# Gate scatter of a product-key expert layer: one-hots for two tokens side by side in place of four

## The chip, the cores and the metric

The kernel runs on one core of one Trainium2 chip. Its time is the device time of one execution, in microseconds (us); several executions are timed and their median is given. TensorE multiplies matrices, VectorE, ScalarE and GpSimd work element by element, and the SyncE queue issues most of the DMAs. The engines run side by side and wait for one another by semaphores. Each engine works its instructions off in the order in which they stand in its own queue. TensorE first loads a matmul's stationary operand (its weights) and then streams the columns of the moving operand past it; the profile lists the loads apart, as PEld.

## The reference

One residual decoder layer on 256 tokens of 1024 features, in float32: a token-mixing part (two causal attention branches), and a part that retrieves experts by product keys, then a norm. The change concerns the second. Each token has 8 heads; each head scores two sets of 128 sub-keys, and its 16 best pairs of sub-keys name 16 of 128 x 128 experts, with softmax gates. An expert is one neuron:

```
u = expert_u[ic]
hval = jnp.einsum('cd,chkd->chk', xc, u)
a = gc * jax.nn.gelu(hval, approximate=False)
out = jnp.einsum('chk,chkd->cd', a, expert_v[ic])
```

## The kernel before, in words

The kernel gathers no experts. It computes all 16384 neurons for all tokens, and multiplies each by the sum of the gates that its token gave to it, zero for most. The experts lie in 128 blocks of 128, block i holding those whose first sub-key is i. `up(i)` (L446) computes one block for all 256 tokens: a load of 512 KB from `u_t`, a split of these weights into two parts of a rounded four-byte type (`hi` on ScalarE, L83, and `lo` on VectorE, L84), and 24 matmuls of 128 x 128 weights with 256 columns (three products for each of eight slices of the features, L93, L96, L97). The last stage, `v_step`, multiplies the gated neurons with `v_e`, 128 blocks of 12 matmuls with 512 columns each.

The gates come from `route` (L456), which picks the experts on VectorE while the query projections and the first 42 blocks of `up` (`N_PRE`) run on TensorE. It leaves for each token its 128 slots (8 heads of 16) across the partitions: `slot_e` holds the two sub-key numbers of a slot, `slot_g` its gate as the sum of two fp16 numbers, a high and a low part.

`scatter(t4, done)` (L595) turns the slots of four tokens into a matrix of gates, 128 second sub-keys by 128 first ones for each token. On VectorE it compares `iota`, the numbers 0 to 127, with the slots of the four tokens at once; that gives both one-hots in `oh` (L602), and `gi` (L603) is the first one-hot times the two parts of the gate. Both tiles are [128, 2, 128, 4] in fp16: the four tokens lie innermost, next to each other, so the 128 columns of one token lie four elements, 8 bytes, apart. On TensorE each token takes two matmuls (L606), with `oh[:, 1, :, q]` as weights and `gi[:, part, :, q]` as the moving operand: 128 x 128 by 128 columns, eight for a scatter, into one PSUM bank. The bank is then multiplied into the neurons that are already there (L608, L611 on VectorE), or copied for those that come later (L613 on ScalarE), which `up_post` (L617) multiplies by the neuron afterwards (L624, L625).

There are 64 scatters (256 tokens in fours). They are called between the blocks 42 to 127 of `up`, about three for every four blocks, and those are the stretch from 388 to 697 us of the profile. Pools of two buffers each hold `oh`, `gi` and the PSUM banks; weights have three. The order within each engine's queue is laid down when the kernel is built, by the framework's scheduler from a modelled timeline, so a scatter's eight matmuls need not stand together in TensorE's queue.

Of the kernel before, what the change touches and what calls it, by code (L numbers as in the profile page):

```python
# [11 lines left out]
F16 = mybir.dt.float16  # L12
# [3 lines left out]
ALU = mybir.AluOpType  # L16
AX = mybir.AxisListType

P = 128
# [10 lines left out]
NK = 128  # L30
# [11 lines left out]
C_ID, C_IOTA, C_POS, C_KEEP = np.cumsum([0, P, P, NCAND]).tolist()  # L42
# [9 lines left out]
def body(ctx, tc, x, g_mix, w_fb, w_va, w_qk, w_gate, w_f, b_f, w_br, w_out, g_ffn, w_pq,  # L52
         keys_t, u_t, v_e, g_fin, c_keep, c_mix, c_rot, c_sel, out, dbg=None):
    nc = tc.nc
# [8 lines left out]
    def bank(tag):  # L63
        return psum.tile([P, 512], F32, name=tag)
# [34 lines left out]
    cst = cpool.tile([P, C_KEEP], F32, name="cst")  # L99
# [67 lines left out]
    def proj_t(src, xt, behind=None, tag="mm", late=False):  # L167
        w = split(src, behind)
        ps = bank(tag)[:, :S]
        if not late:  # L170
            for k in range(KD):
                mm3(ps, wk(w, k), [v[:, k] for v in xt], k == 0, k == KD - 1)
        else:

            for k in range(KD):
                for v in xt:
                    nc.tensor.matmul(ps, lhsT=wk(w, k)[0], rhs=v[:, k], start=k == 0 and v is xt[0], stop=False)  # L177
            for k in range(KD):
                nc.tensor.matmul(ps, lhsT=wk(w, k)[1], rhs=xt[0][:, k], start=False, stop=k == KD - 1)
        return ps  # L180


    with ExitStack() as fr:
# [5 lines left out]
        for t in range(NT):  # L189
            for n in range(2):  # L190
                sl = slice(n * 512, (n + 1) * 512)
# [23 lines left out]
        ps = bank("tp")[:HEADS, :S]  # L215
# [17 lines left out]
        for o in (0, 32, 64):  # L233
            part = ck[o:o + HEADS, P:]
# [149 lines left out]
        for j2 in range(KD // 2):  # L384
# [3 lines left out]
            for jj in range(2):  # L388
                j = 2 * j2 + jj
                pp = []  # L390
                for w, yt, tag in ((wb, ys[0], "mm"), (wa, ys[1], "py")):
                    ps = bank(tag)[:, :S]
# [40 lines left out]
    tk = ctx.enter_context(tc.tile_pool(name="tk", bufs=1))  # L433

    slot_e = tk.tile([P, 2, S], F16, name="slot_e")
    slot_g = tk.tile([P, 2, S], F16, name="slot_g")
    iota = tk.tile([P, NK, 4], F16, name="iota")
    nc.vector.tensor_copy(out=iota, in_=cst[:, C_IOTA:C_IOTA + P].unsqueeze(2).to_broadcast([P, NK, 4]))
    ew = ctx.enter_context(tc.tile_pool(name="ew", bufs=2))
    pre = ctx.enter_context(tc.tile_pool(name="pre", bufs=1))  # L440
    act = [pre.tile([P, N_PRE, S], F32, name="act0")]
# [109 lines left out]
    with ExitStack() as fr:  # L551
# [21 lines left out]
        for m in range(2 * PH):  # L573
            first = m < FIRST
            ps = proj_t(w_pq[m], xt2, (None if m == 0 else normed[0], normed[1]) if first else (qhs[m - FIRST], None), late=first)
# [19 lines left out]
    def scatter(t4, done):  # L595

        ps = bank("tp")
        sl = slice(t4 * 4, t4 * 4 + 4)
        wide = [P, 2, NK, 4]
        oh = ew.tile(wide, F16, name="oh")  # L600
        gi = ew.tile(wide, F16, name="gi")
        nc.vector.tensor_tensor(out=oh, in0=iota.unsqueeze(1).to_broadcast(wide), in1=slot_e[:, :, sl].unsqueeze(2).to_broadcast(wide), op=ALU.is_equal)  # L602
        nc.vector.tensor_tensor(out=gi, in0=oh[:, 0].unsqueeze(1).to_broadcast(wide), in1=slot_g[:, :, sl].unsqueeze(2).to_broadcast(wide), op=ALU.mult)  # L603
        for q in range(4):
            for part in range(2):
                nc.tensor.matmul(ps[:, q * NK:(q + 1) * NK], lhsT=oh[:, 1, :, q], rhs=gi[:, part, :, q], start=part == 0, stop=part == 1)  # L606
        pv = ps.rearrange("p (q i) -> p i q", i=NK)
        nc.vector.scalar_tensor_tensor(out=act[0][:, :, sl], in0=pv[:, :N_PRE], scalar=1.0 / G_SCALE, in1=act[0][:, :, sl], op0=ALU.mult, op1=ALU.mult)  # L608
        d = done - N_PRE
        if d > 0:  # L610
            nc.vector.scalar_tensor_tensor(out=act[1][:, :d, sl], in0=pv[:, N_PRE:done], scalar=1.0 / G_SCALE, in1=act[1][:, :d, sl], op0=ALU.mult, op1=ALU.mult)  # L611
        if done < NK:
            nc.scalar.mul(out=act[1][:, d:, sl], in_=pv[:, done:], mul=1.0 / G_SCALE)  # L613
# [15 lines left out]
    t4 = 0  # L629
    for i in range(N_PRE, NK):  # L630
        upto = -(-(i - N_PRE + 1) * n4 // (NK - N_PRE))
        while t4 < upto:
            scatter(t4, i)
            t4 += 1
        up_post(i, 4 * t4)
# [63 lines left out]
    for n, lo in enumerate((0, 256, 512, 768)):  # L699
        sl = slice(lo, lo + 256)  # L700
# [85 lines left out]
```

## Time and profile before

| | |
|---|---|
| time, median of 3 runs | 1054.86 us (1054.21 to 1056.71) |
| profiled execution | 1059.37 us, its span 1057.6 us |
| TensorE matmuls | busy 1040.5 us (98%), 7076 instructions |
| VectorE | busy 740.6 us (70%), 1479 instructions |
| ScalarE | busy 546.1 us (52%), 983 instructions |
| HBM | 167 GB/s over the span |

The span reaches from the first instruction to the last. Busy times are shares of it; matmuls overlap in their pipeline, so the length of one is more than the time from its start to the start of the next. "Idle before" is the time in which an engine stood still ahead of the instructions of a row, with what it waited for behind the arrow.

### The profile page before, as it was taken

How to read it: one execution, taken by the hardware profiler on the slowest of the kernel's cores; microseconds unless marked ns; L12 is line 12 of the kernel's file. 1: busy time of each engine (PE TensorE's matmuls, PEld its weight loads, DVE VectorE, ACT ScalarE, POOL GpSimd, SP SyncE). 2: the span in 40 equal slices, each digit the busy share in tenths (PEclk: the TensorE clock that was granted, in tenths of full speed). 3: DMA queues.
4: the chain of work that ended last, by engine and by line, in shares of the span. 5: the costliest groups of instructions: out<-in, count | busy, mean ns of one | idle time of the engine just before them, and what ended most of it. 6: DMA issues, size and time to landing. Idle time of an engine off the chain costs nothing.

```text
span 1057.6 us, 18493 instructions
## 1 busy us (share of the span) xinstructions
PE 1040.5 (98%) x7076; PEld 953.7 (90%) x7076; DVE 740.6 (70%) x1479; ACT 546.1 (52%) x983; POOL 6.9 (1%) x12
## 2 busy tenths in 40 slices
PE   7999999989999999999999999999999999999997
PEld 5888999989999999999999999998888888888886
DVE  4566546679999986677777788866566656656665
ACT  5555566454554544444444444455555555555554
POOL 1000000000000000000000000000000000000001
PEclk8999999999999999999999999999999999999999
DMA  6544435544566564545455444556666666666663
GB/s 206 172 139 118 123 120 175 186 169 151 167 190 189 177 186 150 158 142 155 146 151 149 146 152 142 157 163 197 189 193 198 192 190 195 196 190 193 198 193 126
DMA packets 49959, 177.84 MB, mean 168 GB/s; under 512 B 5752, under 2 KB 6648, under 8 KB 49744
## 3 DMA queue, kind: packets, MB, share of 16 engines
q1 hardware_dynamic: 49104, 175.62, 54.9%
q8 instruction: 55, 0.90, 0.4%
q10 hardware_dynamic: 432, 0.66, 0.2%
q0 software_dynamic: 336, 0.40, 0.2%
q14 instruction: 32, 0.26, 0.1%
HBM read 175.60 MB, written 1.05 MB: 167 GB/s over the span
## 4 chain that ended last, share of the span: by engine, by line
PE 95%; DVE 3%; DMA 1%; ACT 0%; issue 0%; SPq 0%; ACTq 0%
PE mm L93 16%; PE mm L96 15%; PE mm L97 15%; PE py L93 6%; PE py L97 6%; PE py L96 6%; PE tp L606 6%; PE sp L93 6%; PE sp L97 6%; PE sp L96 6%; PE sp L312 1%; PE mm L177 1%; DVE lo L84 1%; DMA cst<-in_c_keep_dram 1%; PE sp L580 1%; PE tp L327 1%
## 5 line engine op out<-in xcount | busy, mean ns | idle before, releaser
L84 DVE TENSOR_TENSOR lo<-raw,hi 128x1024 fp32r<-128x1024 f32 x328 | 400.2, 1221 | 145.7 <-ACT hi L83 143.8
L83 ACT CAST hi<-raw 128x1024 fp32r<-128x1024 f32 x328 | 344.8, 1053 | 256.2 <-PE mm L96 142.0
L93 PE MATMUL mm<-xt2h,hi 128*128 128x256 f32 x1128 | 325.8, 289 | 0.8 <-ACT act L588 0.8
L97 PE MATMUL mm<-xt2h,lo 128*128 128x256 f32 x1128 | 317.5, 281 | 0.5 <-DVE lo L84 0.5
L96 PE MATMUL mm<-xt2l,hi 128*128 128x256 f32 x1128 | 317.2, 281 | 0.0
L93 PEld LDWEIGHTS mm<-xt2h,hi 128*128 128x128 f32 x1128 | 214.3, 190 | 1.6 <-ACT act L588 1.0
L97 PEld LDWEIGHTS mm<-xt2h,lo 128*128 128x128 f32 x1128 | 212.7, 189 | 0.9 <-DVE lo L84 0.9
L96 PEld LDWEIGHTS mm<-xt2l,hi 128*128 128x128 f32 x1128 | 213.6, 189 | 0.0
L643 ACT CAST ah<-act 128x256 fp32r<-128x256 f32 x128 | 52.0, 407 | 95.2 <-PE sp L96 95.1
L644 DVE TENSOR_TENSOR al<-act,ah 128x256 fp32r<-128x256 f32 x128 | 54.3, 425 | 60.0 <-PE sp L97 59.1
L96 PE MATMUL py<-lo,ah 128*128 128x512 f32 x256 | 79.9, 390 | 0.0
L93 PE MATMUL py<-hi,ah 128*128 128x512 f32 x256 | 79.7, 390 | 0.0
L97 PE MATMUL py<-hi,al 128*128 128x512 f32 x256 | 79.6, 389 | 0.0
L96 PE MATMUL sp<-lo,ah 128*128 128x512 f32 x254 | 79.0, 389 | 0.0
L93 PE MATMUL sp<-hi,ah 128*128 128x512 f32 x254 | 78.9, 389 | 0.0
L97 PE MATMUL sp<-hi,al 128*128 128x512 f32 x254 | 78.7, 389 | 0.0
L606 PE MATMUL tp<-gi,oh 128*128 128x128 f16 x512 | 74.8, 296 | 0.0
L613 ACT ACTIVATE act<-tp 128x344 f32<-128x344 f32 (+31 forms) x64 | 20.3, 318 | 86.6 <-DVE act L611 80.8
L608 DVE SCALAR_TENSOR_TENSOR act<-tp,act 128x168 f32<-128x168 f32 x64 | 21.2, 332 | 56.1 <-PE tp L606 56.1
L93 PE MATMUL mm<-xt1h,hi 128*128 128x256 f32 x208 | 60.4, 290 | 0.0
L97 PE MATMUL mm<-xt1h,lo 128*128 128x256 f32 x208 | 59.5, 286 | 0.0
L96 PE MATMUL mm<-xt1l,hi 128*128 128x256 f32 x208 | 59.3, 285 | 0.0
(259 smaller groups left out, 1408.0 us busy)
## 6 DMA issues: line engine op xcount, KB each, us to landing
raw<-in_u_t_dram SPq DMA_DIRECT2D x128, 512.0 KB, 3.5
raw<-in_v_e_dram SPq DMA_DIRECT2D x128, 512.0 KB, 3.5
raw<-in_w_gate_dram SPq DMA_DIRECT2D x16, 512.0 KB, 3.6
raw<-in_w_pq_dram SPq DMA_DIRECT2D x16, 512.0 KB, 3.7
raw<-in_w_fb_dram SPq DMA_DIRECT2D x8, 512.0 KB, 4.7
raw<-in_w_va_dram SPq DMA_DIRECT2D x8, 512.0 KB, 3.5
raw<-in_w_qk_dram SPq DMA_DIRECT2D x8, 512.0 KB, 3.6
raw<-in_w_br_dram SPq DMA_DIRECT2D x8, 512.0 KB, 3.5
```

Of the source, the lines that this page charges most:

```text
L83: ih = nc.scalar.copy(out=h, in_=r)
L84: il = nc.vector.tensor_tensor(out=l, in0=r, in1=h.bitcast(F32), op=ALU.subtract)
L93: i = nc.tensor.matmul(ps, lhsT=lhs[0], rhs=rhs[0], start=start, stop=False)
L96: nc.tensor.matmul(ps, lhsT=lhs[0], rhs=rhs[1], start=False, stop=False)
L97: return nc.tensor.matmul(ps, lhsT=lhs[1], rhs=rhs[0], start=False, stop=stop)
L177: nc.tensor.matmul(ps, lhsT=wk(w, k)[0], rhs=v[:, k], start=k == 0 and v is xt[0], stop=False)
L312: nc.tensor.matmul(sp[:, o:o + n], lhsT=q[:, t * P:(t + 1) * P], rhs=k[:, :n], start=not fox, stop=not fox or t == 1)
L606: nc.tensor.matmul(ps[:, q * NK:(q + 1) * NK], lhsT=oh[:, 1, :, q], rhs=gi[:, part, :, q], start=part == 0, stop=part == 1)
L608: nc.vector.scalar_tensor_tensor(out=act[0][:, :, sl], in0=pv[:, :N_PRE], scalar=1.0 / G_SCALE, in1=act[0][:, :, sl], op0=ALU.mult, op1=AL ...
L613: nc.scalar.mul(out=act[1][:, d:, sl], in_=pv[:, done:], mul=1.0 / G_SCALE)
L643: nc.scalar.copy(out=ah, in_=at(i))
L644: nc.vector.tensor_tensor(out=al, in0=at(i), in1=ah.bitcast(F32), op=ALU.subtract)
```

## The change

The tiles of one-hots and gate products hold two tokens in place of four, so each scatter makes two `oh` and two `gi` of 512 elements in a partition in place of one of 1024 each, with four buffers of each kind in place of two. The columns of one token now lie two elements, 4 bytes, apart. The matmuls are as many as before and have the same shapes; the first two tokens of a scatter read the first pair of tiles and the others the second. `iota` is repeated twice in place of four times.

```diff
-    iota = tk.tile([P, NK, 4], F16, name="iota")
-    nc.vector.tensor_copy(out=iota, in_=cst[:, C_IOTA:C_IOTA + P].unsqueeze(2).to_broadcast([P, NK, 4]))
+    iota = tk.tile([P, NK, 2], F16, name="iota")
+    nc.vector.tensor_copy(out=iota, in_=cst[:, C_IOTA:C_IOTA + P].unsqueeze(2).to_broadcast([P, NK, 2]))
...
-        wide = [P, 2, NK, 4]
-        oh = ew.tile(wide, F16, name="oh")
-        gi = ew.tile(wide, F16, name="gi")
-        nc.vector.tensor_tensor(out=oh, in0=iota.unsqueeze(1).to_broadcast(wide), in1=slot_e[:, :, sl].unsqueeze(2).to_broadcast(wide), op=ALU.is_equal)
-        nc.vector.tensor_tensor(out=gi, in0=oh[:, 0].unsqueeze(1).to_broadcast(wide), in1=slot_g[:, :, sl].unsqueeze(2).to_broadcast(wide), op=ALU.mult)
+        wide = [P, 2, NK, 2]
+        ohs, gis = [], []
+        for z in range(2):
+            s2 = slice(t4 * 4 + 2 * z, t4 * 4 + 2 * z + 2)
+            oh = ew.tile(wide, F16, name="oh", bufs=4)
+            gi = ew.tile(wide, F16, name="gi", bufs=4)
+            nc.vector.tensor_tensor(out=oh, in0=iota.unsqueeze(1).to_broadcast(wide), in1=slot_e[:, :, s2].unsqueeze(2).to_broadcast(wide), op=ALU.is_equal)
+            nc.vector.tensor_tensor(out=gi, in0=oh[:, 0].unsqueeze(1).to_broadcast(wide), in1=slot_g[:, :, s2].unsqueeze(2).to_broadcast(wide), op=ALU.mult)
+            ohs.append(oh)
+            gis.append(gi)
         for q in range(4):
             for part in range(2):
-                nc.tensor.matmul(ps[:, q * NK:(q + 1) * NK], lhsT=oh[:, 1, :, q], rhs=gi[:, part, :, q], start=part == 0, stop=part == 1)
+                nc.tensor.matmul(ps[:, q * NK:(q + 1) * NK], lhsT=ohs[q // 2][:, 1, :, q % 2], rhs=gis[q // 2][:, part, :, q % 2], start=part == 0, stop=part == 1)
```

## Rows read from the trace of the kernel before

**Rows 1.** The page: busy time of the engines, and one costly group.

```profile
PE 1040.5 (98%) x7076; PEld 953.7 (90%) x7076; DVE 740.6 (70%) x1479; ACT 546.1 (52%) x983; POOL 6.9 (1%) x12
...
L97 PE MATMUL mm<-xt2h,lo 128*128 128x256 f32 x1128 | 317.5, 281 | 0.5 <-DVE lo L84 0.5
```

**Rows 2.** Chain that ended last, 388 to 697 us: start, length, what.

```profile
by line: PE mm L93 26.8%; PE mm L96 26.7%; PE mm L97 26.6%; PE tp L606 19.9%; PE tp L543 0.1%
...
388.65 0.59 PE tp L606 x5
...
696.06 0.96 PE tp L606 x8
```

**Rows 3.** Busy time by stretch: length, each engine's busy us, clock, DMA.

```profile
342.00:388.00 46.00, 46.00 (x389) 45.87 (x389) 45.53 (x112) 24.23 (x35) 0.00 (x0) 1.00 0.58 176
388.00:697.00 309.00, 309.00 (x2608) 304.72 (x2608) 228.91 (x421) 140.73 (x325) 0.00 (x0) 1.00 0.51 151
600.00:660.00 60.00, 60.00 (x509) 59.17 (x508) 47.83 (x85) 26.22 (x64) 0.00 (x0) 1.00 0.51 150
```

**Rows 4.** Groups by line and shape, 388 to 697 us: busy, mean ns, idle before.

```profile
L84 DVE TENSOR_TENSOR lo<-raw,hi 128x1024 fp32r<-128x1024 f32 x88 | 107.4, 1221 | 21.6 <-ACT hi L83 21.6
...
L606 PE MATMUL tp<-gi,oh 128*128 128x128 f16 x512 | 74.8, 296 | 0.0
L606 PEld LDWEIGHTS <-oh 128*128 128x128 f16 x512 | 49.6, 119 | 4.1
...
L602 DVE TENSOR_TENSOR oh<-iota,slot_e 128x1024 f16<-128x1024 f16 x62 | 42.3, 682 | 2.3 <-PE tp L606 2.3
...
L608 DVE SCALAR_TENSOR_TENSOR act<-tp,act 128x168 f32<-128x168 f32 x63 | 20.8, 332 | 54.5 <-PE tp L606 54.5
```

**Rows 5.** Timeline of TensorE from 482.8 us, matmuls, then weight loads: start, length.

```profile
482.88 0.88 PE L606 MATMUL tp<-gi,oh 128*128 128x128 f16 x6
...
483.73 0.28 PE L96 MATMUL mm<-xt2l,hi 128*128 128x256 f32 x1
483.84 0.29 PE L97 MATMUL mm<-xt2h,lo 128*128 128x256 f32 x1
...
484.20 0.28 PE L97 MATMUL mm<-xt2h,lo 128*128 128x256 f32 x1
...
482.88 0.16 PEld L606 LDWEIGHTS <-oh 128*128 128x128 f16 x2
...
483.47 0.21 PEld L93 LDWEIGHTS mm<-xt2h,hi 128*128 128x128 f32 x1
...
483.73 0.19 PEld L97 LDWEIGHTS mm<-xt2h,lo 128*128 128x128 f32 x1
```

**Rows 6.** Timeline of TensorE's matmuls in the last stage, around 720 us.

```profile
720.23 0.62 PE L96 MATMUL sp<-lo,ah 128*128 128x512 f32 x2
720.68 0.62 PE L97 MATMUL py<-hi,al 128*128 128x512 f32 x2
```

**Rows 7.** Warm-up matmuls: timeline from 5.2 us; loads by line (min/median/max).

```profile
5.02 1.24 PE L200 MATMUL py<-wz 128*128 128x512 f16 x5
...
L200 PEld LDWEIGHTS <-wz x14: 98/152/152, 1.2 to 5.7; 128*128 128x128 f16 x14
L200 PE MATMUL py<-wz x14: 379/622/635, 1.2 to 5.9; 128*128 128x512 f16 x14
```

**Rows 8.** Timeline of TensorE from 388.39 us: the first scatter matmul and its load.

```profile
388.49 0.28 PE L606 MATMUL tp<-gi,oh 128*128 128x128 f16 x1
...
388.38 0.11 PEld L606 LDWEIGHTS <-oh 128*128 128x128 f16 x1
```

**Rows 9.** Groups by line and shape on VectorE, 300 to 388 us.

```profile
L533 DVE TENSOR_TENSOR pr<-oh,ce 128x800 f32<-128x800 f16 x8 | 7.9, 988 | 0.2
...
L530 DVE TENSOR_TENSOR oh<-pkf,posr 128x640 f16<-128x640 f16 x4 | 2.0, 489 | 0.0
```

**Rows 10.** Timeline of VectorE, 487.3 to 490.2 us.

```profile
487.61 0.68 DVE L602 TENSOR_TENSOR oh<-iota,slot_e 128x1024 f16<-128x1024 f16 x1
488.21 1.22 DVE L84 TENSOR_TENSOR lo<-raw,hi 128x1024 fp32r<-128x1024 f32 x1
```

## The prediction, made before the result was known

> **What bounds the kernel now.** I read the page first [rows 1]: TensorE is busy for 98% of the span. So only what changes TensorE's own pace, or makes it wait, can move the end. The chain that ended last, cut to the stretch from 388 to 697 us in which the scatter's matmuls (L606) run, comes next [rows 2]: all of it is TensorE, and 19.9% of the 309 us, 61.5 us, is L606, in 85 unbroken pieces of 2 to 8 matmuls that lie between the `up` matmuls. That is 120 ns for each of the 512. The busy time by stretch [rows 3] says that TensorE works for all 309 us of this stage, at full clock, while VectorE is busy for 228.9 us and ScalarE for 140.7. The groups by line [rows 4] show no idle time of TensorE ahead of L606, and in the whole run it waits 0.5 us for VectorE's L84 [rows 1]. VectorE on the other hand waits 54.5 us for L606's results (L608): it runs ahead of TensorE. So in this stage TensorE's issue rate is the time.
>
> **Why a scatter matmul costs 120 ns.** The timeline gives the pace of each kind. In `up`, 256 columns of four-byte data follow each other at 0.12 us (483.84 to 484.20 is three of them) [rows 5]; in the last stage 512 such columns take 0.227 (two each 0.455) [rows 6]. The difference is 0.42 ns a column, with some 0.011 us on top. The warm-up's matmuls of 512 adjacent fp16 columns, once the clock is up, follow at (1.24 - 0.38) / 4 = 0.215 us, 0.38 being the length of one [rows 7]: again 0.42 ns a column, and hardly anything on top. L606 has only 128 columns, and its pace is (0.88 - 0.296) / 5 = 0.117 us [rows 4, 5], as if it had 256. What differs is the step: both its operands are read 8 bytes apart. Is it the moving operand or the weight load? The first L606 of the stage has its weights requested at 388.38, 0.11 us before it starts, and still lasts 0.28 us [rows 8], just what 256 columns last at 484.20. So I take it that the moving columns are read at half pace: 128 x 0.84 = 107 ns and 0.011 us on top, 0.118.
>
> **The change, part by part.**
>
> *Matmuls.* Their number, shapes and order in the code stay; the columns of both operands now lie 4 bytes apart. Of that step the trace has one example at full pace, the four-byte data of `up`: at its 0.42 ns a column and 0.011 us on top, 128 columns give 0.065 us. The lower end is 0.056, with the overhead of the fp16 row; the upper end is the present 0.118. I take 0.065, since the row with the same step between columns is the nearest. That is 0.053 us less for each matmul whose slot ends with its columns.
>
> *Not all slots do.* The last matmul of a piece is followed by an L93 whose weight load starts with it (483.47, 0.21 us), and the L96 behind that starts at 483.73, 0.26 us after the last L606 [rows 5]. Two `up` slots are 0.24, so the load of the four-byte weights already decides there, and a shorter scatter matmul ahead of it gives nothing. That leaves 512 - 85 = 427 slots: 427 x 0.053 = 22.6 us. With 0.056 it is 26.5, and 28 if the new order leaves every scatter's eight together (448 slots); were every scatter cut into two pieces of four (384 slots), it would be 20.4.
>
> *VectorE.* Two operations of 1024 elements (682 ns) become four of 512. From 640 fp16 elements in 489 ns to 1024 in 682 [rows 4, 9] the slope is 0.50 ns an element. From start to start an operation takes 0.60 us (487.61 to 488.21) [rows 10], so a half takes 0.60 - 512 x 0.50 / 1000 = 0.344, and a scatter 4 x 0.344 against 2 x 0.60: 0.18 us more. For 62 scatters that is 11 us; on 228.9 it makes 240 us of the 286 that remain, 84%. TensorE's own work hides it; if that cover were gone it would cost the 11. The upper bound is the loss of the fp16 pace: L84 takes 1221 ns for 1024 four-byte elements and L533 988 for 800 [rows 4, 9], 1.04 ns an element; 512 of them at that slope and the overhead of `oh` (0.60 - 0.51) are about 0.62 us, a scatter is 1.28 us longer, the stage has 79 more: 308 us of work. I don't take it, since both inputs and the output still end in adjacent fp16 elements, as in the row of 640.
>
> *The repeated slot.* In a half, two adjacent slots, one four-byte word, are repeated for all 128 rows; before it was two words. L533 repeats one four-byte word 8 times in one input and lies on one line with L84, which repeats nothing; the rest beyond 1.04 ns an element is 0.16 us for both [rows 4, 9]. So I add nothing for it. [...]
>
> *The rest.* The smaller `iota` is written once, in a fraction of a microsecond. Between 342 and 388 VectorE is busy for 45.5 of 46 us [rows 3], and the first two scatters' products are made around there: 0.3 us more with hardly any cover, which I count in full. DMAs, PSUM banks and the evictions L608 to L613 are as before, and as many tokens can be in flight. L84 stands behind two small operations more in VectorE's queue; its reader has waited 0.5 us in the whole run. The loads of `u_t` must come in at 309 / 286 of today's 151 GB/s, 163; the stretch ahead ran at 176 with TensorE full [rows 3].
>
> **Sum.** 22.6 - 0.3 = 22.3 us off the span of 1057.6: 1035.3. The profiled execution took 1059.37, 1.8 around its span, which stays; it lies 4.5 above the median of the runs, 1054.86. The stage behind is TensorE's as well, by its 98% of the span, so that it starts and ends earlier by as much: 1054.86 - 22.3, about 1032.5.
>
> **Rivals.**
>
> *The weight load sets the pace.* A load for L606 takes 119 ns on average [rows 4], and the matmuls follow at 117: each could be waiting for its own. Then the step matters only by what it does to the load. The warm-up's load of adjacent fp16 weights takes 98 ns at least [rows 7], so the pace would become 0.100 and the gain 427 x 0.018 = 7.7 us, 1047; or, if the load keeps its length, nothing: 1055. For it speaks that the two lengths agree so well. Against it: in `up` loads of 0.19 us go with a pace of 0.12, so the length of a load is not the pace; two loads of L606 are through within 0.16 us at 482.88 [rows 5]; and the first L606 above is long with its weights there. [...]
>
> *VectorE takes over: slower.* If runs of two elements lose the fp16 pace, VectorE has 308 us of work in a stage that now takes 309. From 600 to 660 us, where L611 and L625 are long, it is busy for 47.8 of 60 us [rows 3]; 12.5 scatters at 1.28 add 16, 64 us: there it decides, and with part of the waits for L608 that are in its queue now (54.5 us) the stage ends up to 20 us late: 1055 to 1075. The late part loses from the point at which a half takes more than 0.55 us, the whole stage from 0.62. Against it: the inner elements stay adjacent.
>
> *Neck and neck.* If a half takes 0.45 to 0.52 us, between the two bounds, VectorE needs some 270 to 285 of the 286 us and, being in order, stalls TensorE now and then: about half the gain, 1041 to 1050. [...]
>
> **Chances.** The matmuls speed up and TensorE stays the bound, 1026 to 1041 (a pace of 0.056 to 0.085): 0.66. The weight load: 0.09 at 1047 and 0.10 at no change. Neck and neck: 0.07. VectorE the bound: 0.08, of which 0.03 ends within 0.3%. Some 0.3% (3 us) is what a measurement of this kernel tells from no change. Faster: 0.66 + 0.09 + 0.07 = 0.82; same: 0.10 + 0.03 = 0.13; slower: 0.05. The range of 1026 to 1050 takes in the first case, the shorter load and the middle case and leaves out the rest.
>
> **What would show it.** Right: a piece of eight L606 takes about 0.6 us in the chain in place of 0.96, with no idle time of TensorE ahead of it; a single L606 lasts about 0.23 us; a half of `oh` or `gi` takes about 425 ns; VectorE is busy for 80 to 87% of the stage, which ends near 675 us. Wrong: a pace of 0.100 or 0.118 and the stage hardly shorter (the load sets it); halves of 0.55 us and more, with TensorE idle ahead of L606 or L97 on VectorE; or the time given back in the last stage, in waits on `v_e`.

## The result, and the profile after

The changed kernel takes 1029.22 us (median; 1027.86 to 1031.06) against 1055.78 in the same rounds: 26.6 us less, a ratio of 0.9749 with a 95% interval of 0.9734 to 0.9764. The prediction was 1032.5 with a range of 1026 to 1050. Two more sets of runs gave 0.9740 (0.9726 to 0.9753) and 0.9747 (0.9731 to 0.9762).

Lines are renumbered by the change: `oh` is now L605, `gi` L606, and the scatter's matmuls are L611. First the page's part 1, then the busy time by stretch (length, then busy us of TensorE, its loads, VectorE, ScalarE and GpSimd, clock, DMA share and GB/s), beside [rows 1] and [rows 3]:

```profile
PE 1012.9 (98%) x7076; PEld 927.5 (90%) x7076; DVE 749.0 (73%) x1607; ACT 542.0 (53%) x983; POOL 6.9 (1%) x12
```

```profile
387.00:669.00 282.00, 282.00 (x2609) 278.94 (x2609) 237.26 (x546) 136.63 (x323) 0.00 (x0) 1.00 0.56 165
...
600.00:660.00 60.00, 60.00 (x563) 59.37 (x562) 54.76 (x124) 27.93 (x71) 0.00 (x0) 1.00 0.57 164
```

TensorE is still busy for the whole stage. VectorE is at 84% of it, and at 91% from 600 to 660 us. The chain that ended last, from the first scatter matmul to the last, answers to [rows 2]:

```profile
by line: PE mm L93 30.5%; PE mm L96 29.3%; PE mm L97 29.3%; PE tp L611 10.9%; PE tp L543 0.1%
387.54 0.29 PE tp L611 x5
...
506.53 0.48 PE tp L611 x8
512.74 0.59 PE tp L611 x10
...
668.18 0.48 PE tp L611 x8
```

A piece of eight counts 0.48 us where it counted 0.96. From the start of the first piece to the end of the last it is 281.1 us; before it was 308.4 (388.65 to 697.02): 27.3 us less, against 26.6 between the medians. The two profiled spans differ by 28.3 (1057.6 and 1029.3); the rest, some 1.1 us, lies ahead of the first scatter matmul, whose start varies as much between runs of one kernel: it is at 387.4 us here, and at 385.1 and 384.2 in two more profiles of the changed kernel. In this chain no engine but TensorE appears, before or after. The timeline around one piece of eight answers to [rows 5]:

```profile
480.36 0.28 PE L97 MATMUL mm<-xt2h,lo 128*128 128x256 f32 x1
480.48 0.64 PE L611 MATMUL tp<-gi,oh 128*128 128x128 f16 x8
480.92 0.36 PE L93 MATMUL mm<-xt2h,hi 128*128 128x256 f32 x1
481.12 0.28 PE L96 MATMUL mm<-xt2l,hi 128*128 128x256 f32 x1
...
480.48 0.46 PEld L611 LDWEIGHTS <-oh 128*128 128x128 f16 x8
480.90 0.19 PEld L93 LDWEIGHTS mm<-xt2h,hi 128*128 128x128 f32 x1
```

Eight matmuls take 0.64 us with the last one's length; from the L97 ahead to the L96 behind it is 0.76 us, 0.52 more than two `up` slots. The groups of the stage (busy, mean ns | idle before, on what), beside [rows 4]:

```profile
L605 DVE TENSOR_TENSOR oh<-iota,slot_e 128x512 f16<-128x512 f16 x124 | 52.0, 420 | 21.8 <-PE tp L611 21.1
L606 DVE TENSOR_TENSOR gi<-oh,slot_g 128x512 f16<-128x512 f16 x124 | 51.7, 418 | 0.2
L611 PE MATMUL tp<-gi,oh 128*128 128x128 f16 x507 | 41.1, 220 | 0.0
L611 PEld LDWEIGHTS <-oh 128*128 128x128 f16 x507 | 29.2, 97 | 3.0
```

One scatter matmul lasts 220 ns (296 before), its weight load 97 (119 before), a half of `oh` or `gi` 418 to 420. TensorE has no idle time ahead of L611.

### The profile page after: what moved, and what is told of

It reads as the page before. It is cut to its first block, busy times and chain, and to the rows that moved or that the text cites. A ratio compares the mean times of both kernels' runs of the same rounds, so it can differ in the third digit from the quotient of the medians.

```text
span 1029.3 us, 18596 instructions
## 1 busy us (share of the span) xinstructions
PE 1012.9 (98%) x7076; PEld 927.5 (90%) x7076; DVE 749.0 (73%) x1607; ACT 542.0 (53%) x983; POOL 6.9 (1%) x12
## 4 chain that ended last, share of the span: by engine, by line
PE 95%; DVE 3%; DMA 1%; ACT 0%; issue 0%; SPq 0%; ACTq 0%
PE mm L93 16%; PE mm L96 16%; PE mm L97 16%; PE py L93 7%; PE py L96 7%; PE py L97 7%; PE sp L96 6%; PE sp L93 6%; PE sp L97 6%; PE tp L611 3%; PE sp L312 1%; PE mm L177 1%; PE sp L580 1%; DVE lo L84 1%; DMA cst<-in_c_keep_dram 1%; PE tp L327 1%
## 5 line engine op out<-in xcount | busy, mean ns | idle before, releaser
L83 ACT CAST hi<-raw 128x1024 fp32r<-128x1024 f32 x328 | 344.6, 1052 | 285.2 <-PE mm L96 171.9
L93 PE MATMUL mm<-xt2h,hi 128*128 128x256 f32 x1128 | 323.7, 287 | 0.8 <-ACT act L588 0.8
L97 PE MATMUL mm<-xt2h,lo 128*128 128x256 f32 x1128 | 317.4, 281 | 0.3 <-DVE lo L84 0.3
L96 PE MATMUL mm<-xt2l,hi 128*128 128x256 f32 x1128 | 317.0, 281 | 0.0
L93 PEld LDWEIGHTS mm<-xt2h,hi 128*128 128x128 f32 x1128 | 212.5, 188 | 1.2 <-ACT act L588 1.0
L97 PEld LDWEIGHTS mm<-xt2h,lo 128*128 128x128 f32 x1128 | 212.4, 188 | 0.5 <-DVE lo L84 0.5
L96 PEld LDWEIGHTS mm<-xt2l,hi 128*128 128x128 f32 x1128 | 212.7, 189 | 0.0
L96 PE MATMUL py<-lo,ah 128*128 128x512 f32 x256 | 79.7, 389 | 0.0
L93 PE MATMUL py<-hi,ah 128*128 128x512 f32 x256 | 79.6, 389 | 0.0
L97 PE MATMUL py<-hi,al 128*128 128x512 f32 x256 | 79.5, 389 | 0.0
L96 PE MATMUL sp<-lo,ah 128*128 128x512 f32 x254 | 79.0, 389 | 0.0
L93 PE MATMUL sp<-hi,ah 128*128 128x512 f32 x254 | 78.9, 389 | 0.0
L97 PE MATMUL sp<-hi,al 128*128 128x512 f32 x254 | 78.6, 389 | 0.0
L605 DVE TENSOR_TENSOR oh<-iota,slot_e 128x512 f16<-128x512 f16 x128 | 53.5, 420 | 21.8 <-PE tp L611 21.1
L93 PE MATMUL mm<-xt1h,hi 128*128 128x256 f32 x208 | 60.4, 290 | 0.0
L97 PE MATMUL mm<-xt1h,lo 128*128 128x256 f32 x208 | 59.5, 286 | 0.0
L96 PE MATMUL mm<-xt1l,hi 128*128 128x256 f32 x208 | 59.2, 285 | 0.0
L97 PEld LDWEIGHTS py<-hi,al 128*128 128x128 f32 x256 | 48.1, 188 | 10.0
L96 PEld LDWEIGHTS py<-lo,ah 128*128 128x128 f32 x256 | 48.1, 188 | 9.9
```

What stands on the lines that cost most here:

```text
L83: ih = nc.scalar.copy(out=h, in_=r)
L93: i = nc.tensor.matmul(ps, lhsT=lhs[0], rhs=rhs[0], start=start, stop=False)
L96: nc.tensor.matmul(ps, lhsT=lhs[0], rhs=rhs[1], start=False, stop=False)
L97: return nc.tensor.matmul(ps, lhsT=lhs[1], rhs=rhs[0], start=False, stop=stop)
```

## The experiments

The theory (M) is that TensorE reads the moving columns at a pace set by their distance in bytes. Its rival (W) is that each matmul waits for its weight load, whose length depends on the distance. Others are that the order of the queues brought the gain, and that VectorE's finer operations took some of it back. "Pace" is the time from one scatter matmul to the next, taken from a piece of eight: its length less that of one, over seven.

**The moving operand alone, and the weights alone.** In e1_moving4 `oh` is made as before and only `gi` in halves; in e2_weights4 the reverse, the halves of `gi` being written into one tile of four.

```diff
# e1_moving4, against the kernel before; half = [P, 2, NK, 2]
-        gi = ew.tile(wide, F16, name="gi")
...
+            gi = ew.tile(half, F16, name="gi", bufs=4)
...   the matmul: lhsT=oh[:, 1, :, q], rhs=gis[q // 2][:, part, :, q % 2]
# e2_weights4, against the changed kernel; wide = [P, 2, NK, 4]
+        gi = ew.tile(wide, F16, name="gi")
...
+            oh = ew.tile(half, F16, name="oh", bufs=4)
...   the matmul: lhsT=ohs[q // 2][:, 1, :, q % 2], rhs=gi[:, part, :, q]
```

> Only the moving operand (gi) has its columns 4 bytes apart; the one-hots, and so the weights, stay 8 bytes apart and are made by one operation for four tokens. Theory M (the step of the moving columns sets the pace): scatter matmuls follow each other at 0.057 to 0.065 us; with 82 pieces in TensorE's order the stage loses some 25 to 27 us, time 1028 to 1033. Theory W (each matmul waits for its weight load, which lasts 117 ns at a step of 8 bytes): the load stays at 117, the pace at 0.118, time 1054 to 1057. If both count: a pace between, 0.08 to 0.10, time 1036 to 1046.

> The mirror image: the one-hots and so the weights lie 4 bytes apart, the moving operand stays 8 bytes apart (its halves are written into one tile by two operations). Theory M: the weight load shortens to 97 ns and the pace stays at 0.107 to 0.118 us, time 1050 to 1057. Theory W: the pace follows the load to 0.058, as in the changed kernel, time 1028 to 1032; or to the load's own 0.100, time 1046 to 1048.

e1_moving4 took 1031.31 us, ratio 0.9776 (0.9760 to 0.9793); e2_weights4 1053.81, ratio 0.9987 (0.9978 to 0.9997). A piece of eight in the timeline of e1_moving4, and then the lengths of all its weight loads (min/median/max):

```profile
435.83 0.66 PE L611 MATMUL tp<-gi,oh 128*128 128x128 f16 x8
```

```profile
L611 PEld LDWEIGHTS <-oh x512: 110/113/138, 384.3 to 668.6; 128*128 128x128 f16 x171
```

The same two of e2_weights4:

```profile
442.42 1.10 PE L611 MATMUL tp<-gi,oh 128*128 128x128 f16 x8
```

```profile
L611 PEld LDWEIGHTS <-oh x512: 96/115/119, 383.7 to 690.6; 128*128 128x128 f16 x171
```

With a weight load of 113 ns the matmuls of e1_moving4 follow at (0.66 - 0.22) / 7 = 0.063 us: the load does not set the pace, and W falls. With the weights 4 bytes apart and the moving columns still at 8, the pace is (1.10 - 0.296) / 7 = 0.115. So nearly all of the gain, 24.5 of 26.6 us, is the moving operand's. The weights' step is worth some 2 us at most: e2_weights4 gains 2.0, between 0.3 and 2.3 by its interval, and of what e1_moving4 lacks some 0.9 goes to the order of TensorE's queue, in which the trace has 84 pieces in place of the changed kernel's 69, at the 0.06 us a piece found below. The loads of e2_weights4 came out at 115 ns where I had expected 97: with the same weights a load lasted longer among slow matmuls than among fast ones, so the agreement of 119 and 117 ns that spoke for W was no evidence. The kernel m16 below parts the two numbers: its loads last 118 ns while its matmuls follow at 0.229 us.

**The halves without the step.**

```diff
...   oh, gi: [P, 2, NK, 4], as before; c = slice(2 * z, 2 * z + 2)
+            nc.vector.tensor_tensor(out=oh[:, :, :, c], ...)
+            nc.vector.tensor_tensor(out=gi[:, :, :, c], ...)
```

> VectorE works in halves of two tokens exactly as in the changed kernel, but writes them into tiles of four, so both operands stay 8 bytes apart. Theory M, and W as well (the step is all): pace 0.118 us, VectorE's halves at 420 ns add some 11 us of work that TensorE hides, time 1053 to 1057. Rival (the gain comes from the finer operations, which let the scheduler order TensorE's and VectorE's queues in another way): 1028 to 1035.

1055.08 us, ratio 0.9993 (0.9983 to 1.0003). Its groups from 390 to 660 us:

```profile
L610 PE MATMUL tp<-gi,oh 128*128 128x128 f16 x445 | 64.4, 296 | 0.0
L607 DVE TENSOR_TENSOR gi<-oh,slot_g 128x512 f16<-128x512 f16 x112 | 45.1, 417 | 0.0
```

VectorE's four operations in place of two cost nothing here and bring nothing, and a scatter matmul lasts 296 ns as before. The order of the queues is another in this kernel than in the changed one (79 pieces against 69), so that it alone doesn't exclude the rival of the order; e7_merged, below, does: it has the pieces of the kernel before, two buffers as before and one operation for four tokens, and yet the whole gain.

**The law of the step.** The moving columns 16, 12 and 6 bytes apart, by tiles of which a part is not used. One execution each.

```diff
# m16, m12 (on the kernel before): W = 8, 6; the reads of gi stay
-        gi = ew.tile(wide, F16, name="gi")
+        gi = ew.tile([P, 2, NK, W], F16, name="gi", bufs=1)[:, :, :, :4]
# m6 (on the changed kernel)
-            gi = ew.tile(wide, F16, name="gi", bufs=4)
+            gi = ew.tile([P, 2, NK, 3], F16, name="gi", bufs=2)[:, :, :, :2]
```

> The kernel before with the moving columns 16 bytes apart (tile of eight of which four are used, one buffer in place of two); weights stay 8 bytes apart. Theory M, linear (the read passes 4 bytes of address a column time of 0.42 ns, whatever it uses of them): 128 x 1.68 ns + 0.011 = 0.226 us a matmul, 512 x 0.108 = 55 us more, time about 1110. Theory M, saturated (beyond 8 bytes each column is one read already): 0.118 and about 1055. Theory W: the load stays at 117, so 0.118 and 1055 too.

> The kernel before with the moving columns 12 bytes apart (rows of six of which four are used, one buffer in place of two), weights 8 bytes apart; 67 pieces. Even rate: 128 x 1.26 + 0.011 = 0.172 us, 512 x 0.054 = 28 us more than before, time about 1083. If a step counts as the next multiple of 8 bytes: 0.231 as at 16 bytes, 1112. At 16 bytes the rate came out at 1.71 ns a column, 4.1 times that of four-byte data.

> The changed kernel with the moving columns 6 bytes apart (products of two tokens in rows of three, two buffers in place of four), weights 4 bytes apart; 90 pieces. If the read passes address at an even rate (4 bytes in 0.42 ns): 128 x 0.63 + 0.011 = 0.092 us a matmul, 512 x 0.092 + 90 x 0.06 = 52.5 us of scatter against 61.5 before, time about 1047. If a step counts as the next multiple of 8 bytes: 0.118 us, 1055. If only the elements fetched count up to 8 bytes: 0.058, 1029. A half of gi written in rows 6 bytes apart may lose the fp16 pace on VectorE (0.68 in place of 0.42 us), which TensorE would still hide for the most part.

They took 1112.75, 1083.93 and 1043.19 us; the kernel before took 1055.77 (median) beside the first and 1056.50 (one execution) beside the other two. A piece of eight in the timeline of m16 (one of its matmuls lasts 409 ns), the L96 behind it, and the lengths of its weight loads:

```profile
426.95 2.01 PE L606 MATMUL tp<-gi,oh 128*128 128x128 f16 x8
...
428.92 0.28 PE L96 MATMUL mm<-xt2l,hi 128*128 128x256 f32 x1
```

```profile
L606 PEld LDWEIGHTS <-oh x512: 112/118/138, 384.5 to 750.3; 128*128 128x128 f16 x171
```

the same of m12 (352 ns):

```profile
423.92 1.57 PE L606 MATMUL tp<-gi,oh 128*128 128x128 f16 x8
...
425.44 0.28 PE L96 MATMUL mm<-xt2l,hi 128*128 128x256 f32 x1
```

and of m6 (252 ns):

```profile
438.98 0.86 PE L611 MATMUL tp<-gi,oh 128*128 128x128 f16 x8
...
439.82 0.28 PE L96 MATMUL mm<-xt2l,hi 128*128 128x256 f32 x1
```

| bytes between moving columns | 4 | 6 | 8 | 12 | 16 |
|---|---|---|---|---|---|
| pace, us | 0.060 | 0.087 | 0.117 | 0.174 | 0.229 |

From 4 to 16 bytes the pace is in proportion to the step, some 0.0145 us for each byte of 128 columns. In that range it neither rounds up to 8 nor stops growing. The weights lie 4 bytes apart in the columns for 4 and 6, and 8 bytes in the others; at 4 bytes with the weights 8 apart e1_moving4 had 0.063. In m6's groups from 390 to 660 us `gi`, written in rows 6 bytes apart, is dearer on VectorE, and TensorE still doesn't wait:

```profile
L606 DVE TENSOR_TENSOR gi<-oh,slot_g 128x512 f16<-128x512 f16 x117 | 69.6, 595 | 32.7 <-PE tp L611 32.3
L611 PE MATMUL tp<-gi,oh 128*128 128x128 f16 x465 | 54.0, 252 | 0.0
```

**Adjacent columns.** One token after the other, so that the slot is repeated within the row.

```diff
+        wide = [P, 2, 4, NK]
+        ... in1=slot_e[:, :, sl].unsqueeze(3).to_broadcast(wide), op=ALU.is_equal)
...   the matmul: lhsT=oh[:, 1, q], rhs=gi[:, part, q]
```

> Columns adjacent, 2 bytes apart: one token after the other, so the slot is repeated along the innermost row on VectorE. Theory: TensorE gains nothing more by it, 0.056 to 0.058 us a matmul, 66 pieces. VectorE loses the fp16 pace: 1024 elements in about 1.22 us each for one-hots and products, 62 x 1.08 = 67 us more than before in the stage, 296 of some 281: VectorE becomes the bound, TensorE waits for gi or lo; time 1042 to 1060. Rival (the repeated slot keeps the fp16 pace): 0.68 us an operation, TensorE the bound, time 1028 to 1031.

1058.18 us, ratio 1.0026 (1.0013 to 1.0039). Its groups, and its stretches:

```profile
L603 DVE TENSOR_TENSOR gi<-oh,slot_g 128x1024 f16<-128x1024 f16 x62 | 75.5, 1218 | 0.0
L602 DVE TENSOR_TENSOR oh<-iota,slot_e 128x1024 f16<-128x1024 f16 x62 | 75.4, 1217 | 0.9 <-PE tp L606 0.9
```

```profile
388.00:697.00 309.00, 286.86 (x2615) 279.95 (x2614) 291.67 (x422) 136.09 (x325) 0.00 (x0) 1.00 0.50 151
600.00:660.00 60.00, 54.14 (x490) 52.54 (x491) 58.48 (x81) 24.29 (x63) 0.00 (x0) 1.00 0.46 141
```

A piece of eight in its timeline, and the longest wait of TensorE (in total, times, longest):

```profile
432.93 0.62 PE L606 MATMUL tp<-gi,oh 128*128 128x128 f16 x8
```

```profile
PE mm L93 <- ACT hg L624: 22.0, 19, 1.7
```

ScalarE's queue around one of these waits, which ends when an L93 starts at 644.72:

```profile
643.28 1.04 ACT L83 CAST hi<-raw 128x1024 fp32r<-128x1024 f32 x1 [2.07 <-PE mm L96]
644.23 0.20 ACT L621 ACTIVATE act<-mm 128x40 f32<-128x40 f32 x1
644.33 0.34 ACT L624 ACTIVATE hg<-mm 128x212 f32<-128x212 f32 x1
```

TensorE's pace is 0.057 us, hardly better than the 0.060 at 4 bytes. VectorE has lost the fp16 pace, 1218 ns in place of 682, and is busy for 58.5 of 60 us in the late part. Its 291.7 us of work are more than the changed kernel's whole stage of 281.1, so that this layout could not have kept that stage. TensorE stands still for 22 us more. Its records name ScalarE's L624, the reading of the PSUM bank. In each of the 19 waits L624 stands shortly behind an L83 that had itself waited for 1.3 to 3.0 us; where the trace names a cause for that, in five of them, it is TensorE's own L96. So these waits run through the order of ScalarE's queue, and the trace does not show that VectorE's longer operations lead to them. The prediction's slower rival is made real here in VectorE's work, by another layout, and only in part in the time.

**VectorE's operations, and the number of pieces.** In e7_merged the slots are stored in the order pair, part, token, so one operation serves four tokens with the columns still 4 bytes apart; its TensorE queue has the same 85 pieces as the kernel before, where the changed kernel has 69. e8_pairs is the same with two scatters called together, 44 pieces.

```diff
+    slot_e = tk.tile([P, S // 2, 2, 2], F16, name="slot_e")
...
+        oh = ew.tile([P, 2, 2, NK, 2], F16, name="oh")
+        nc.vector.tensor_tensor(out=oh.rearrange("p z e k q -> p (z e) k q"), ...)
# e8_pairs besides
-        while t4 < upto:
+        while t4 + 1 < upto or (i == NK - 1 and t4 < upto):
             scatter(t4, i)
-            t4 += 1
+            scatter(t4 + 1, i)
+            t4 += 2
```

> The changed kernel once more, beside the next ones on the same chip: 1028 to 1031 us, 26 to 27 below the kernel before, 69 pieces of scatter matmuls, 0.0575 us each.

> Columns 4 bytes apart as in the changed kernel, but one operation of 1024 elements each for the one-hots and the products of four tokens, as before (the slots are stored in the order pair, part, token, so that one access pattern covers both pairs). TensorE's queue has the very pieces of the kernel before, 85. Theory (the step is all, a piece costs 67 ns beside its matmuls): 512 x 0.0575 + 85 x 0.067 = 35.1 us of scatter on TensorE against 34.1 with 69 pieces: 1.1 us slower than the changed kernel, some 25.5 below the kernel before. VectorE is busy for about 11 us less than in the changed kernel, and that shows nowhere. Rival (VectorE's extra operations cost the changed kernel something): 1 to 5 us faster than it.

> As the merged kernel, with the scatters called two at a time, so that TensorE's queue has 44 pieces, half of them of 16. If a piece costs 67 ns beside its matmuls: 512 x 0.0575 + 44 x 0.067 = 32.4 us, 1.7 us less than the changed kernel, 2.7 less than the merged one. Rival: the evictions of two PSUM banks in a row hold TensorE up, or the weight loads behind a longer piece come late: no gain, or a loss of 1 to 5 us.

1028.04, 1029.25 and 1025.81 us; ratios to the kernel before 0.9740, 0.9745 (0.9732 to 0.9758) and 0.9721 (0.9707 to 0.9734). e7_merged has less for VectorE to do, 230 us from 388 to 670 us against 238, and is not faster: VectorE's extra operations cost nothing that the runs can tell. Whether it is slower by its 16 pieces the intervals don't tell, but the chain does. Its first and last pieces:

```profile
384.68 0.29 PE tp L609 x5
...
666.37 0.48 PE tp L609 x8
```

That is 282.2 us from the first to the last, 26.2 less than the kernel before with the same pieces, and 1.1 more than the changed kernel with its 69. e8_pairs was run against the changed kernel once more:

> The changed kernel beside the paired one, on the same chip and in the same rounds, to tell their difference: 1026.5 to 1030.

> The paired kernel (44 pieces against 69). If a piece costs 67 ns, 25 fewer give 1.7 us: 1024 to 1028, 1 to 3 below the changed kernel in the same rounds. Rival (the 2.2 us seen before was scatter of the runs): equal medians.

1028.10 and 1025.57. Over both sets, ten executions each, the means are 1028.34 and 1026.13, 2.2 us apart, give or take 1.1 (95%). The paired kernel lies below both others, by about what 25 pieces at 0.06 to 0.07 us give. Two of its pieces in the chain:

```profile
439.34 0.94 PE tp L609 x16
446.01 0.48 PE tp L609 x8
```

Eight more matmuls in a piece are 0.46 us, 0.0575 for one: that is the pace without what a piece's ends cost. (The 0.060 of the table has the first matmul of the piece in it.)

## Why the prediction was right, and where its sizes were off

*The mechanism.* TensorE bounds the stage, its moving columns were read at half pace, and 4 bytes remove that: shown by e1_moving4 against e2_weights4 and e3_halves8, by e7_merged, and by the row of steps. At 8 bytes the pace is 0.117 us, at 4 it is 0.060.

*The pace.* I had 0.065, the columns of `up` at 0.42 ns and its 0.011 us on top. It is 0.0575. At 0.42 ns a column that leaves 0.004 us on top, where `up` has 0.011 at the same step; the fp16 row of the warm-up [rows 7] was the nearer one for it. (I tied that row's faster matmuls to the clock; the granted clock reads 1.00 in each microsecond from 1 to 6, over those of 622 ns and those of 379 alike. The row's 0.215 us does not rest on it.) But the 0.053 of gain for a slot was too small for some and too large for others. Averaged over all pieces of the two traces, from start to start, the second matmul of a piece follows the first at 0.070 us in place of 0.108, 0.038 less, and the later ones follow at 0.0575 in place of 0.118, 0.061 less. With the old 85 pieces that is 85 x 0.038 + 342 x 0.061 = 24.1 us for the 427 slots, against the 22.6 of the sum.

*"Not all slots do."* This step failed. I read the 0.26 us from the last L606 to the L96 behind it as the four-byte weight load's, which a shorter matmul could not help. After the change the last L611 starts at 480.48 + 0.64 - 0.22 = 480.90, and the L96 at 481.12: 0.22 us. Over all pieces the mean was 0.255 and is 0.228. In e2_weights4, with the moving columns at 8 bytes, it stays at 0.256, and in e1_moving4 it is 0.230, so it is the moving operand's. In m6 it is 0.232 (the piece above: 438.98 + 0.86 - 0.25 = 439.59 to 439.82), in m12 0.309 and in m16 0.364. There is a floor of about 0.23 us, then, but at 8 bytes the slow columns still lay above it: 85 x 0.027 = 2.3 us that I had written off. That the floor is the weight load's is not shown.

*The order.* I gave the case in which the new order keeps a scatter's eight together, but summed with the old 85 pieces. The scheduler made 69. A piece costs 0.52 - 8 x 0.0575 = 0.06 us beside its matmuls, 16 of them 1.0 us.

*The sum.* 24.1 for the slots, 2.3 for the last ones and 1.0 for the order are 27.4; the stage gained 27.3, where the sum had 22.6. The time of 1029.22 is only 3.3 us from the forecast 1032.5, though the gain of 26.6 is 4.3 us more than the forecast 22.3, because the kernel before came to 1055.78 in the set with one more run, and not to 1054.86.

*VectorE.* Forecast were 425 ns for a half and 240 us in the stage; measured 418 to 420 and 237. The repeated word cost nothing, as L533 had said: the 425 ns count nothing for it, and the halves came out below them. The route stage's 0.3 us can't be told in the runs.

*The rivals.* The weight load is refuted: in e1_moving4 loads of 113 ns go with a pace of 0.063 us. VectorE as the bound, and neck and neck, did not happen at 4 bytes: a half took 418 to 420 ns, and TensorE had no idle time ahead of L611. e4_adjacent, with adjacent columns, took 1058 us where 1055 to 1075 was given for it; but it has 291.7 us of VectorE's work and not 308, and waits of TensorE through ScalarE's queue, so that the price is not confirmed by it.

## What to carry to other kernels

Look at the pace of a matmul, start to start, against its number of columns, and at what lies between those columns in bytes: here 128 columns at 8 bytes cost as much as 256 adjacent four-byte ones (0.117 and 0.12 us). The operand that streams was the one to pack, with 24.5 of the 26.6 us; the weights' step mattered little, 2.0 us. A layout that suits TensorE can cost the engine that writes it: with adjacent columns VectorE took 1218 ns for 1024 fp16 elements in place of 682. Two fp16 elements side by side were the point at which VectorE kept its fp16 pace (418 to 420 ns for 512) and TensorE nearly all of its own (0.060 us against 0.057).

## What was not expected of the hardware

- The pace of moving fp16 columns is in proportion to their distance from 4 to 16 bytes (0.060 to 0.229 us for 128; at 6, 12 and 16 bytes by one execution each), and at 2 bytes hardly better than at 4 (0.057).
- Weights 8 bytes apart cost little: 113 ns a load and 0.063 us a matmul, against 97 and 0.060.
- On VectorE rows of two fp16 elements keep the fp16 pace when written side by side (420 ns for 512), and when written 8 bytes apart (417, e3_halves8), but at a distance of 6 bytes a half took 595 ns.
